# A decoder layer on one core: attention values moved in front of later scores, row sums of two halves grouped, five short reorderings

## Chip, cores and metric

The kernel runs on one core of a Trainium2 chip. The time is the device time of one execution in microseconds (us), lower is better; a comparison is made over the median of several runs of each kernel on the same chip. The core has five engines that run their own queues in order: PE (matmuls; PEld is its weight load), DVE (vector), ACT (scalar), POOL and SP, the last two used mainly to issue transfers. PE writes its results to PSUM, eight banks of 2 KB in each of 128 partitions; DVE and ACT read them there.

## What is computed

One layer of a decoder for 512 tokens of width 1024, batch 1, all in float32. Cut to what matters:

```
mod = silu(c) @ w_ada + b_ada                 # 6 rows of 1024: shift, scale, gate for two halves of the layer
h = rmsnorm(x) * (1 + scale1) + shift1
q, k, v, qd, kd, vd, ga, gd = split(h @ w_in)
out_a = sliding-window attention, 8 heads in blocks of 128, sink term in the softmax, ALiBi
out_d = differential attention, 4 heads, two softmax maps each, per-head rmsnorm
merged = sigmoid(ga) * (out_a @ w_branch_swa) + sigmoid(gd) * (out_d @ w_branch_diff)
x = x + gate1 * (merged @ w_out)
h2 = rmsnorm(x) * (1 + scale2) + shift2
a, g = split(h2 @ w_up);  a = causal depthwise conv of width 3 of a
x = x + gate2 * ((gelu(a) * g) @ w_down)
return rmsnorm(x) * final_g
```

## The kernel before

**Precision.** Most products are made from a high part and a low part of each operand (three matmuls in place of one). The high part is a cast on ACT, the low part a subtraction on DVE (`split`, `cast_w` and `low_w`). So each weight block costs one DMA, one ACT and one DVE instruction before PE can use it. `raw`, `whi` and `wlo` tiles have a few buffers each and are given back when their readers are done.

**Who orders what.** A planner orders the instructions of each engine from the program's order, priorities and estimated durations, and picks the buffer of each tile. Inside `manual_schedule` the named engines keep the program's order. PE is held so through the whole of attention, while DVE and ACT are not; from the end of the output projection (L1283) to L1480 all four of PE, DVE, ACT and POOL are held, and again in `last_rows` at the very end.

**Attention.** PE's program is a line of projection steps (`fill(n)` runs n steps; a step is three matmuls of 512 columns) with the pieces of attention set in between at fixed places. Sliding heads are worked two at a time, as pairs 0 to 3, by the loop at L843: scores of the next pair (`swa_scores`), transpositions of this pair's probabilities in two halves (`swa_transpose`, one for each head of the pair, each in two tiles), softmax of the next pair on DVE and ACT (`swa_softmax`), then the values of this pair (`swa_values`). The values are sixteen matmuls `oa` (L606); ACT (L428) and DVE (L429) take the result out of PSUM into `outa`. Scores end in DVE's reduction (L561), softmax in DVE's scaling of the probabilities by the inverse sums (L584), which the transpositions read (L595).

**PSUM banks.** Four tags: `f` (2 banks, projections), `s` (3, scores), `t` (2, transpositions, row sums and small things), `v` (1, values, and the second scores of the second half in a pair). A tile waits until the former user of its bank has been read.

**Modulation rows.** `ada_rows` makes four of the six rows of `mod` beside attention, with one 512 KB load each eighth fill step: DVE multiplies weight rows by silu(c) and adds them up in an accumulator `arow` (L776, L778), one for each half of a row. When a half is complete, `ada_spread` sums it over the partitions by four column groups of matmuls with ones (`pr`, L789), ACT copies the result (`row`, L794) and POOL issues the write to `mod_rows` in memory (L795). Later steps read the rows from there.

**Up projection.** `w_up` is applied in a scheme with seven products in place of eight (names `p1`, `p2`, `p3`, `p4`, `m5`, `m6`, `m7`) for each pair J of column blocks. `mul_slot(J, name)` is a product of 24 matmuls (L1150), `sum_w` makes a sum of weights on DVE in place, `cast_w` and `low_w` make its high and low part, `behind(J, name)` takes a product out of PSUM, and `conv_bias`, `conv_taps` and `conv_gelu` do the convolution: ACT, then two DVE operations, then ACT. For J = 0, 1 and the begin of 2 the order is written out by hand (L1368 to L1479), from J = 2 on a loop runs over the slots. In front of it, `turn2` transposes normalised rows into the two `t` banks, and `mod_one` (ACT) reads them into `b12` and `b22`.

**Down projection and end.** The same scheme in passes over `w_down`, each with six groups of weights and two row blocks u = 0, 1 (`multiply(i, g, u)`, L1759). The pass `m7` and the last pass `p4` add into the same two banks; between the two, DVE reads the banks (L1633). The last three groups of `p4` are in `last_rows`: block 0 completely, block 1 in two halves of columns `c0` and `c1`, and then the final rmsnorm of the two blocks: multiply, add, squares on ACT, inverse root (`rstd_start` on DVE and POOL, `rstd_end` on DVE), scale, store.

Of the kernel before, what the change touches and what calls it, by code (L numbers as in the profile page):

```python
# [14 lines left out]
P = 128  # L15
# [38 lines left out]
def kernel(  # L54
# [47 lines left out]
    def vbank(name):  # L102
        return bank("v", 1, [P, S], name)
# [410 lines left out]
    def after(n, fn):  # L514
        later.append([n, fn])
# [82 lines left out]
        c.pT.append(pt)  # L598

    def swa_values(i):  # L600
        o = vbank(f"oa{i}")
        for kb in (0, 2, 1, 3):
            w = P if kb == 3 else 2 * P
            for j in range(2):
                rows = slice(64 * j, 64 * j + 64)
                nc.tensor.matmul(  # L606
                    o[rows, kb * P : kb * P + w], va[:, kb, rows],
                    pairs[i].pT[j][:, kb * 256 : kb * 256 + w],
                    start=kb == 0, stop=kb == 3, tile_position=(0, 64 * j),
                )  # L610
        with tc.high_priority(offset=HP):
            evac(outa[0][:, i], outa[1][:, i], o)
# [144 lines left out]
    def ada_load(idx, hf, k):  # L757
        c0 = (2 + idx) * D + hf * S
        r = raw_tile([P, 2, S], f"ra{idx}{hf}_{k}")
        nc.sync.dma_start(r, wada[k * P : (k + 2) * P, c0 : c0 + S].rearrange("(a p) n -> p a n", p=P))  # L760
        return r


    def ada_rows():
        todo = [(idx, hf, k) for idx in range(4) for hf in range(2) for k in range(0, KT, 2)]
        r = ada_load(*todo[0])
        yield
        for (idx, hf, k), job in zip(todo, todo[1:] + [None]):
            nxt = ada_load(*job) if job else None
            if k == 0:  # L770
                ac = big.tile([P, S], F32, tag=("sq2", "g2b1")[hf], name=f"arow{idx}{hf}")
            with tc.high_priority(offset=HP // 2) if tick[0] > ADA_EASY else ExitStack():
                for a in range(2):
                    cc = cs[:, k + a : k + a + 1]
                    if k + a == 0:
                        nc.vector.tensor_scalar_mul(ac, r[:, a], cc)  # L776
                    else:
                        nc.vector.scalar_tensor_tensor(ac, r[:, a], cc, ac, ALU.mult, ALU.add)  # L778
            if k == KT - 2:
                after(ADA_LAG, lambda idx=idx, hf=hf, ac=ac: ada_spread(idx, hf, ac))  # L780
            r = nxt
            yield


    def ada_spread(idx, hf, ac):
        pr = tbank(f"pr{idx}{hf}", (P, P))
        for g in range(4):
            gs = slice(32 * g, 32 * g + 32)
            nc.tensor.matmul(  # L789
                pr[gs], ones[:, gs], ac[:, g * P : (g + 1) * P], start=True, stop=True, tile_position=(0, 32 * g)  # L790
            )
        row = big.tile([P, P], F32, tag="g2b0", name=f"row{idx}{hf}")
        with tc.high_priority(offset=HP):
            nc.scalar.copy(row, pr)  # L794
        nc.gpsimd.dma_start(  # L795
            mod_rows[idx, hf * S : (hf + 1) * S].rearrange("(g n) -> g n", g=4), row[0:P:32]
        )


    pair_w = {}  # L800
# [42 lines left out]
    for i in range(SWA_PAIRS):  # L843
        more = i + 1 < SWA_PAIRS
        fill(SWA_FILL[3])
        if more:
            swa_scores(i + 1, range(NT))
        swa_transpose(i, 0)
        fill(SWA_FILL[4])
        swa_transpose(i, 1)  # L850
        fill(SWA_FILL[5])
        if more:
            with tc.issue_after(pairs[i].copied.ins):
                swa_softmax(i + 1)
        fill(SWA_FILL[6])
        swa_values(i)
        fill(SWA_FILL[7])
    while units or loaded or current:
        fill(1)
# [397 lines left out]
    def ks(g):  # L1257
        return slice(2 * (g % 2), 2 * (g % 2) + 2)
# [108 lines left out]
    g22 = pairs2.rearrange("p (b u n) -> p b u n", b=2, u=2)  # L1367
    tps = {g: turn2(2, g) for g in (0, 1)}  # L1368
    mul_slot(0, "p2", (0,))
    cast_w(0, "m5")  # L1370
    for g in (0, 1):
        for kk in range(2):
            mod_one(b12[:, ks(g)], tps[g], g, kk)
    for g in (2, 3):
        tps[g] = turn2(2, g)
    mul_slot(0, "p2", (1,))
    mul_slot(1, "p1", (1,))
    mul_slot(1, "p2")
    bV += [tbank("up6"), tbank("up7")]
    low_w(0, "m5")  # L1380
    for q in (q0, q1):
        V.tensor_sub(t1n[:, q], b11[:, q], b12[:, q])
    sum_w(0, "m6")
    hi_t(0, t1n, q0)
    for kk in range(2):
# [47 lines left out]
    mul_slot(1, "m6")  # L1433
    behind(1, "m5")
    conv_bias(0, 1)
    conv_taps(0, 0)
    sum_w(1, "p3")
    conv_taps(0, 1)
    cast_w(1, "p3")
    conv_gelu(0, 0)  # L1440
    behind(1, "m6")
    cast_w(1, "m7")
    low_w(1, "p3")
    mul_slot(1, "p3")
    conv_gelu(0, 1)
    low_w(1, "m7")
# [2 lines left out]
    cast_w(2, "p1")  # L1449
    behind(0, "c22")  # L1450
    behind(0, "p4")
    behind(1, "p2")
    low_w(2, "p1")
    mul_slot(2, "p1")
    behind(1, "p3")
    cast_w(1, "p4")
# [238 lines left out]
    def last_rows(todo):  # L1695
        man = ExitStack()
        man.enter_context(
            tc.manual_schedule(engines={nc.vector.engine, nc.scalar.engine, nc.tensor.engine, nc.gpsimd.engine})
        )
        c0, c1 = slice(0, H), slice(H, S)  # L1700
        part = [partial(parts[2 + u, 1]) for u in range(2)]
        for g in todo:
            multiply(len(passes) - 1, g, 0)
        for sl in (c0, c1):
            for g in todo:
                multiply(len(passes) - 1, g, 1, sl)
        for u in range(2):
            nc.scalar.activation(x1[:, u], x1[:, u], AF.Copy, scale=stat_end(u))
            nc.sync.dma_start(od[u * P : (u + 1) * P, :], x1[:, u])
        last_mul(0)  # L1710
        s0 = last_add(0)
        last_gain(0)
        last_mul(1, c0)
        r0 = rstd_start(s0, 1, D, bp, plus=part[0])
        s1 = last_add(1, c0)
        last_gain(1, c0)
        rs0 = bp.tile([P, 1], F32, tag="rs2", bufs=4, name="rse0")
        rstd_end(rs0, *r0, 1, bp)
        partial(s1, part[1])
        last_mul(1, c1)  # L1720
        s2 = last_add(1, c1)
        r1 = rstd_start(s2, 1, D, bp, plus=s1)
        last_gain(1, c1)
        last_scale(0, rs0)
        last_scale2(0, rs0, nc.sync)
        rs1 = bp.tile([P, 1], F32, tag="rs2", bufs=4, name="rse1")
        rstd_end(rs1, *r1, 1, bp)
        last_scale(1, rs1)
        last_scale2(1, rs1, nc.scalar)
        man.close()  # L1730
# [37 lines left out]
    for i in range(len(passes)):  # L1768
        for g in range(NG):
            prepare(i, g)  # L1770
            for _ in range(EACH.get(i, (0,) * NG)[g]):
                next(tasks)()
        tail = HOLD if i == len(passes) - 1 else 0
        for g in range(NG - tail):
            for u in range(2):
                multiply(i, g, u)
        if tail:
            last_rows(range(NG - tail, NG))
        else:
            tasks = after_pass(passes[i][0])  # L1780
            if i < 2:
                for _ in tasks:
                    pass
# [27 lines left out]
```

## Time and profile before

| | us |
|---|---|
| median of 3 runs | 704.18 (704.02 to 706.19) |
| profiled execution | 704.88 |
| its span, first to last instruction | 703.0 |
| PE busy | 683.2 (97%) |
| PE's weight loads busy | 595.3 (85%) |
| DVE busy | 571.9 (81%) |
| ACT busy | 375.5 (53%) |
| POOL busy | 82.3 (12%) |

The profile is of one execution. Its rows give the start in us from the begin of the span, the length, the engine, the line of the kernel, the operation, the tile written and the tiles read, the shape and a count of merged instructions; a bracket gives the engine's idle time in front of the row and what ended it. Matmuls overlap, so the length of one is more than its share of PE's time; the distance of starts is what counts. Rough places in time: norm and the sliding heads' projection to 60 us, sliding heads to 119, differential heads, gates and merge to 316, output projection to 362, up projection to 588, down projection to 694, end to 703.

### The profile page before, as it was taken

The page shows a single profiled execution, that of the slowest core. Times are in us where ns is not written, and L with a number is a line of the kernel's source. Part 1 is how long each engine was busy: PE and PEld are TensorE (multiplying, and loading weights), DVE is VectorE, ACT ScalarE, POOL GpSimd, SP SyncE. Part 2 cuts the span into 40 slices and gives each one's busy share as a digit, 9 for nine tenths or more (in the row PEclk, how much of TensorE's full clock was granted, in tenths as well). Part 3 has the DMA queues.
Part 4 walks back from the last instruction along what each step waited for, and adds up shares of the span by engine and source line. Part 5 has one row for each costly group of instructions (what it writes and reads, how often), then busy time and mean ns, then how long its engine had stood idle before and what let it go on. Part 6 is the DMA issues. An engine that isn't in the chain of part 4 may idle for free. (4 is left out here: it accounts for less than half of the span.)

```text
span 703.0 us, 11254 instructions
## 1 busy us (share of the span) xinstructions
PE 683.2 (97%) x4203; PEld 595.3 (85%) x4203; DVE 571.9 (81%) x1098; ACT 375.5 (53%) x668; POOL 82.3 (12%) x100
## 2 busy tenths in 40 slices
PE   6999999999999999999999999999999999999994
PEld 5777776778788888888889999999999999888884
DVE  5899886887885557664589898888888999979996
ACT  3646767455452333331468566655565666656664
POOL 3000000001001000000030111111111102530300
PEclk9999999999999999999999999999999999999998
DMA  9885454354435676229517798786889647996803
GB/s 312 282 260 174 150 151 151 92 170 128 134 108 158 194 225 202 96 106 275 185 44 149 188 212 204 169 206 194 197 213 231 156 148 204 196 198 192 157 1 119
DMA packets 115862, 121.81 MB, mean 173 GB/s; under 512 B 4383, under 2 KB 93280, under 8 KB 115808
## 3 DMA queue, kind: packets, MB, share of 16 engines
q1 hardware_dynamic: 96894, 95.09, 42.5%
q0 software_dynamic: 18720, 25.73, 21.7%
q8 instruction: 33, 0.54, 0.3%
q10 hardware_dynamic: 194, 0.28, 0.1%
q14 instruction: 21, 0.17, 0.1%
HBM read 118.97 MB, written 2.11 MB: 172 GB/s over the span
## 5 line engine op out<-in xcount | busy, mean ns | idle before, releaser
L1150 PE MATMUL up<-t,m_whi 128*128 128x256 f32 x528 | 96.1, 283 | 0.0
L1150 PEld LDWEIGHTS up<-t,m_whi 128*128 128x128 f32 x528 | 82.4, 192 | 0.0
L1150 PE MATMUL up<-t,m_wlo 128*128 128x256 f32 x264 | 74.7, 283 | 0.1
L1150 PE MATMUL up<-bh,p_wlo 128*128 128x256 f32 x232 | 65.7, 284 | 0.6 <-DVE p_wlo L1093 0.6
L1150 PE MATMUL up<-bh,p_whi 128*128 128x256 f32 x232 | 65.6, 283 | 0.0
L1150 PE MATMUL up<-bl,p_whi 128*128 128x256 f32 x232 | 65.6, 283 | 0.0
L778 DVE SCALAR_TENSOR_TENSOR arow<-ra,cs,arow 128x512 f32<-128x512 f32 x56 | 41.9, 748 | 21.7 <-DMA ra<-in_w_ada_dram 21.3
L1150 PEld LDWEIGHTS up<-t,m_wlo 128*128 128x128 f32 x264 | 50.6, 192 | 0.3 <-DVE m_wlo L1093 0.3
L1150 PEld LDWEIGHTS up<-bh,p_wlo 128*128 128x128 f32 x232 | 44.4, 192 | 1.0 <-DVE p_wlo L1093 1.0
L1150 PEld LDWEIGHTS up<-bl,p_whi 128*128 128x128 f32 x232 | 44.5, 192 | 0.0
L1150 PEld LDWEIGHTS up<-bh,p_whi 128*128 128x128 f32 x232 | 44.5, 192 | 0.0
L1061 POOL DMA_DIRECT2D s<-in_w_up_dram x21 | 27.0, 1360 | 143.2 <-DMA s<-in_w_up_dram 80.9
L1093 DVE TENSOR_TENSOR m_wlo<-s,m_whi 128x1024 fp32r<-128x1024 f32 x31 | 37.7, 1218 | 2.0 <-ACT m_whi L1089 2.0
L1089 ACT CAST m_whi<-s 128x1024 fp32r<-128x1024 f32 x31 | 32.4, 1046 | 9.4 <-DVE s L1083 5.9
L1150 PE MATMUL up<-t,p_whi 128*128 128x256 f32 x176 | 32.2, 283 | 0.0
L173 POOL TENSOR_TENSOR r<-ms,mhalf 128x1 f32<-128x1 f32 (+1 forms) x16 | 12.6, 788 | 134.3 <-DVE ms L171 75.7
L795 POOL DMA_DIRECT2D mod_rows<-row x8 | 5.1, 643 | 196.7 <-ACT row L794 196.7
L1150 PEld LDWEIGHTS up<-t,p_whi 128*128 128x128 f32 x176 | 27.4, 192 | 0.2 <-issue 0.2
L698 ACT ACTIVATE sd<-sd,dmx 128x128 f32<-128x128 f32 (+3 forms) x32 | 17.7, 556 | 18.5 <-DVE dmx L690 18.5
L1157 ACT ACTIVATE gT<-a,cv 128x512 f32<-128x512 f32 x22 | 17.7, 813 | 17.7 <-DVE a L1192 17.3
L1089 ACT CAST p_whi<-wa 128x1024 fp32r<-128x1024 f32 x18 | 18.7, 1040 | 12.0 <-PE up L1150 10.8
L1150 PE MATMUL up<-t,p_wlo 128*128 128x256 f32 x88 | 24.9, 283 | 0.0
(473 smaller groups left out, 2054.1 us busy)
## 6 DMA issues: line engine op xcount, KB each, us to landing
ra<-in_w_ada_dram SPq DMA_DIRECT2D x32, 512.0 KB, 3.9
wa<-in_w_up_dram SPq DMA_DIRECT2D x22, 512.0 KB, 4.1
s<-in_w_up_dram SPq DMA_DIRECT2D x21, 512.0 KB, 4.8
s<-in_w_up_dram POOLq DMA_DIRECT2D x21, 512.0 KB, 7.8
adaw<-in_w_ada_dram SPq DMA_DIRECT2D x16, 512.0 KB, 5.3
w<-in_w_in_dram SPq DMA_DIRECT2D x12, 512.0 KB, 4.0
a<-in_w_up_dram SPq DMA_DIRECT2D x11, 512.0 KB, 4.6
b<-in_w_down_dram SPq DMA_DIRECT2D x10, 512.0 KB, 3.5
```

Of the source, the lines that this page charges most:

```text
L173: nc.gpsimd.tensor_tensor(r0, ms, mhalf[:, :n], ALU.pow)
L698: exp = nc.scalar.activation(pm[m], pm[m], AF.Exp, bias=mx[:, m : m + 1], scale=slope, accum_out=lsum[:, m : m + 1])
L778: nc.vector.scalar_tensor_tensor(ac, r[:, a], cc, ac, ALU.mult, ALU.add)
L795: nc.gpsimd.dma_start(mod_rows[idx, hf * S : (hf + 1) * S].rearrange("(g n) -> g n", g=4), row[0:P:32])
L1061: nc.gpsimd.dma_start(dst, upblock(*blk), accum_op=ALU.add)
L1089: nc.scalar.copy(W[J, name][0], R[J, SRC[name]])
L1093: nc.vector.tensor_sub(lo, R[J, SRC[name]], hi.bitcast(F32))
L1150: nc.tensor.matmul(o[u], w[:, k, cu], b[:, k], start=name in ("p1", "m5", "p2") and k == 0 and x == 0, stop=k == 3 and x == 2, skip_group_ ...
L1157: nc.scalar.activation(grow(j), av[J][:, u], AF.Identity, bias=cv[:, 66 + j : 67 + j], scale=cv[:, 44 + j : 45 + j])
```

## The change

Values of pairs 0 and 1 are issued one turn of the loop later, directly in front of the scores of pairs 2 and 3 (two pairs on), and those of pair 2 directly in front of pair 3's. All but the last go to a `t` bank. `ada_spread` waits for both halves of a row and sums them in one group of sixteen matmuls into one bank, with one copy of twice the width and two writes. Five stretches are put in another order: around the first modulations and `cast_w(0, "m5")`; the sum, high and low part of `p3` of J = 1; the low part of `p1` of J = 2; the end's operations; and the last two groups of pass `m7`, which go over u = 0 first and then over u = 1.

```diff
     def swa_values(i):
-        o = vbank(f"oa{i}")
+        o = (vbank if i == SWA_PAIRS - 1 else tbank)(f"oa{i}")
...
         todo = [(idx, hf, k) for idx in range(4) for hf in range(2) for k in range(0, KT, 2)]
+        sums = [None, None]
...
-            if k == KT - 2:
-                after(ADA_LAG, lambda idx=idx, hf=hf, ac=ac: ada_spread(idx, hf, ac))
+            sums[hf] = ac
+            if hf and k == KT - 2:
+                after(ADA_LAG, lambda idx=idx, acs=tuple(sums): ada_spread(idx, acs))
...
-    def ada_spread(idx, hf, ac):
-        pr = tbank(f"pr{idx}{hf}", (P, P))
-        for g in range(4):
-            gs = slice(32 * g, 32 * g + 32)
-            nc.tensor.matmul(
-                pr[gs], ones[:, gs], ac[:, g * P : (g + 1) * P], start=True, stop=True, tile_position=(0, 32 * g)
-            )
-        row = big.tile([P, P], F32, tag="g2b0", name=f"row{idx}{hf}")
+    def ada_spread(idx, acs):
+        pr = tbank(f"pr{idx}", (P, 2, P))
+        for hf, ac in enumerate(acs):
+            for g in range(4):
+                gs = slice(32 * g, 32 * g + 32)
+                nc.tensor.matmul(
+                    pr[gs, hf], ones[:, gs], ac[:, g * P : (g + 1) * P], start=hf == 0, stop=hf == 1,
+                    tile_position=(0, 32 * g), skip_group_check=True,
+                )
+        row = big.tile([P, 2, P], F32, tag="g2b0", name=f"row{idx}")
         with tc.high_priority(offset=HP):
             nc.scalar.copy(row, pr)
-        nc.gpsimd.dma_start(
-            mod_rows[idx, hf * S : (hf + 1) * S].rearrange("(g n) -> g n", g=4), row[0:P:32]
-        )
+        for hf in range(2):
+            nc.gpsimd.dma_start(
+                mod_rows[idx, hf * S : (hf + 1) * S].rearrange("(g n) -> g n", g=4), row[0:P:32, hf]
+            )
...
         if more:
+            if i:
+                swa_values(i - 1)
             swa_scores(i + 1, range(NT))
...
-        swa_values(i)
+        if not more:
+            swa_values(i - 1)
+            swa_values(i)
...
     mul_slot(0, "p2", (0,))
-    cast_w(0, "m5")
     for g in (0, 1):
         for kk in range(2):
             mod_one(b12[:, ks(g)], tps[g], g, kk)
+        if g == 0:
+            cast_w(0, "m5")
...
+    V.tensor_sub(t1n[:, q0], b11[:, q0], b12[:, q0])
     low_w(0, "m5")
-    for q in (q0, q1):
-        V.tensor_sub(t1n[:, q], b11[:, q], b12[:, q])
+    V.tensor_sub(t1n[:, q1], b11[:, q1], b12[:, q1])
...
     conv_bias(0, 1)
+    sum_w(1, "p3")
     conv_taps(0, 0)
-    sum_w(1, "p3")
+    cast_w(1, "p3")
+    low_w(1, "p3")
     conv_taps(0, 1)
-    cast_w(1, "p3")
     conv_gelu(0, 0)
     behind(1, "m6")
     cast_w(1, "m7")
-    low_w(1, "p3")
...
     behind(0, "p4")
+    low_w(2, "p1")
     behind(1, "p2")
-    low_w(2, "p1")
...
         last_gain(0)
-        last_mul(1, c0)
         r0 = rstd_start(s0, 1, D, bp, plus=part[0])
-        s1 = last_add(1, c0)
-        last_gain(1, c0)
         rs0 = bp.tile([P, 1], F32, tag="rs2", bufs=4, name="rse0")
         rstd_end(rs0, *r0, 1, bp)
-        partial(s1, part[1])
+        last_scale2(0, rs0, nc.sync)
+        last_mul(1, c0)
+        s1 = last_add(1, c0)
         last_mul(1, c1)
         s2 = last_add(1, c1)
+        last_scale(0, rs0)
+        partial(s1, part[1])
         r1 = rstd_start(s2, 1, D, bp, plus=s1)
+        last_gain(1, c0)
         last_gain(1, c1)
-        last_scale(0, rs0)
-        last_scale2(0, rs0, nc.sync)
...
         tail = HOLD if i == len(passes) - 1 else 0
-        for g in range(NG - tail):
+        twins = 2 if i == len(passes) - 2 else 0
+        for g in range(NG - tail - twins):
             for u in range(2):
+                multiply(i, g, u)
+        for u in range(2):
+            for g in range(NG - tail - twins, NG - tail):
                 multiply(i, g, u)
```

## The prediction, made before the changed kernel was seen

> **What bounds the kernel now.** I first read the table of stretches (busy time of each engine, with counts), since it says where a gain can still lie.
>
> ```profile
> 60.00:120.00 60.00, 59.15 (x397) 45.53 (x396) 51.12 (x161) 39.25 (x113) 0.77 (x1) 1.00 0.50 153
> 120.00:360.00 240.00, 239.90 (x1202) 193.89 (x1201) 165.67 (x340) 94.68 (x185) 14.58 (x19) 1.00 0.50 155
> 360.00:420.00 60.00, 58.97 (x478) 57.55 (x477) 56.05 (x86) 43.59 (x72) 10.52 (x9) 1.00 0.74 165
> 420.00:660.00 240.00, 240.00 (x1722) 227.60 (x1721) 215.28 (x306) 143.28 (x210) 47.75 (x42) 1.00 0.83 194
> 660.00:703.00 43.00, 33.87 (x163) 28.16 (x161) 35.33 (x64) 23.63 (x40) 2.36 (x4) 0.93 0.23 69
> ```
>
> The columns after the length are PE, PEld, DVE, ACT, POOL, then the granted clock. PE is the bound from 60 us to the end of its work: it is busy 59.15 of 60, 239.90 of 240, 58.97 of 60 and 240.00 of 240 us, at full clock. What can be won before 694 us is therefore PE's small waits (0.85 us in 60-120, 1.03 us in 360-420) and whatever makes PE take longer for the same matrix work. DVE is second, and in 360-420 it is close (56.05 of 60). Behind PE's last matmul lies a chain of other engines up to the end; there the bound is latency. I then read PE's timeline around every place the diff touches, and after it DVE and ACT there.
>
> **Row sums in one group.** One island of eight small matmuls (four column groups, two passes) stands between projection matmuls:
>
> ```profile
> 108.82 0.40 PE L121 MATMUL pw<-hThA,w_l 128*128 128x512 f32 x1
> 109.14 0.43 PE L789 MATMUL pr<-arow,ones 128*32 128x128 f32 x8
> ...
> 109.83 0.39 PE L120 MATMUL pw<-hTlA,w_h 128*128 128x512 f32 x1
> 110.06 0.40 PE L121 MATMUL pw<-hThA,w_l 128*128 128x512 f32 x1
> ```
>
> Projection matmuls start 0.23 us apart (109.83 to 110.06). From 108.82 to 109.83 are two such steps plus the island: 1.01 - 0.46 = 0.55 us, most of which is getting in and out. There are eight islands now (2 halves x 4 rows) and four of double size afterwards. The added eight matmuls cost at least nothing and at most the 0.43 us that eight take from first start to last end; I take the middle, 0.22, because four of the eight overlap in one pass. New: 4 x 0.77 = 3.08 us, old: 8 x 0.55 = 4.40 us. Term **-1.3** (bounds -2.2 and -0.5). The copies fall from eight to four, each wider, on an ACT that has 145 of 240 us free; the eight write-outs stay eight, two at a time on POOL's queue, which is busy 0.77 of 60 us, then 14.58 of 240. Their first reader is the gate row after attention; if that cover went, two queued issues would cost a microsecond there. The first accumulator is now held until the second is full, so the next row's first product on DVE has one ada step of room, not five; at this pace that is eight fill steps, and I count it at nothing.
>
> **Values in front of the scores.** First the price of such a group alone, then joined to scores, then scores alone:
>
> ```profile
> 79.00 0.39 PE L121 MATMUL pw<-hThA,w_l 128*128 128x512 f32 x1
> ...
> 81.31 0.40 PE L120 MATMUL pw<-hTlA,w_h 128*128 128x512 f32 x1
> ...
> 116.77 0.40 PE L121 MATMUL pw<-hThB,w_l 128*128 128x512 f32 x1
> 117.09 1.73 PE L606 MATMUL oa<-pT,va 128*64 128x256 f32 x16
> ...
> 119.98 0.40 PE L120 MATMUL pga<-hTlA,wga_h 128*128 128x512 f32 x1
> ...
> 138.71 0.40 PE L121 MATMUL pA<-outah,wba_l 128*128 128x512 f32 x1
> ...
> 140.26 0.40 PE L120 MATMUL pA<-outal,wba_h 128*128 128x512 f32 x1
> ```
>
> Alone: 81.31 - 79.00 - 0.46 = 1.85 us. Last pair, whose scores follow directly: 119.98 - 116.77 - 0.46 = 2.75, less scores alone 140.26 - 138.71 - 0.46 = 1.09, makes 1.66. Joining is worth 0.19, and three groups get joined (pairs 0 and 1 to scores, pair 2 to pair 3): **-0.57** (bounds 0 and -0.8).
>
> [...]
>
> **The two waits next to it.** The values leave PSUM's single v bank by ACT and then DVE, and the next scores need that bank:
>
> ```profile
> 84.60 1.79 PE L126 MATMUL sw<-ka,qa 64*128 64x128 f32 x24
> 86.33 0.87 PE L595 MATMUL tp<-ident,st 128*128 128x128 f32 x6
> ...
> 97.41 1.07 PE L126 MATMUL sw<-ka,qa 64*128 64x128 f32 x13
> ...
> 99.60 0.98 PE L595 MATMUL tp<-ident,st 128*128 128x128 f32 x7
> ...
> 111.45 0.40 PE L121 MATMUL pw<-hThA,w_l 128*128 128x512 f32 x1
> 112.49 0.65 PE L595 MATMUL tp<-ident,st 128*128 128x128 f32 x4 [0.64 <-ACT row L794]
> ```
>
> The scores at 97.41 take 2.19 us to the next transposition, those at 84.60 took 1.73: 0.46 lost. The transpositions at 112.49 stand 1.04 behind the last matmul, where 0.23 is normal: 0.81 lost, because one of the two t banks still held row sums. Both causes go: **-1.27**. What is late next is the softmax of the last pair:
>
> ```profile
> 108.29 1.07 DVE L584 TENSOR_SCALAR st<-st,lsum 128x128 f32<-128x128 f32 x4
> ...
> 111.67 0.34 DVE L584 TENSOR_SCALAR st<-st,lsum 128x256 f32<-128x256 f32 x1
> ```
>
> Those transpositions were due at 111.68. Ahead of them vanish pair 2's values (1.85), one row-sum island (0.55), 0.38 for two joined groups and the 0.46: due at 108.44, while DVE ends the scaling that they read at 108.29 + 1.07 = 109.36. That gives a new wait of 0.92; the second half ends at 112.01 and may add some 0.4, or, if DVE gets its scores sooner, both shrink to nothing. **+0.9** (bounds 0 and +1.6).
>
> **The new price, a t bank held by values.** Transpositions of the same pair come 1.7 us behind the values now, and their second bank is the one with the values in it:
>
> ```profile
> 83.43 0.49 DVE L776 TENSOR_SCALAR arow<-ra,cs 128x512 f32<-128x512 f32 x1 [1.73 <-DMA ra<-in_w_ada_dram]
> ...
> 84.70 0.66 DVE L429 TENSOR_TENSOR outal<-oa,outah 128x512 fp32r<-128x512 f32 x1
> ```
>
> Before, pair 0's values ended at about 81.0 and DVE released their bank at 84.70 + 0.66 = 85.36, over 4 us later, behind a row product that sat 1.73 us for its DMA. Scores (1.73) and one transposition group (0.44) cover 2.2 us of such a lag, twice (pairs 0 and 1). In the new place ACT is idle and the DVE wait at 83.43 already over, so ACT's copy and DVE's subtraction, some 1.3 us, fit: **0**, with 2 x 2.1 us if the lag stays as it was (a rival below). What queues behind a late subtraction on DVE is the score reduction, which feeds the next softmax.
>
> **Reorderings around the up projection.**
>
> ```profile
> 368.36 1.23 DVE L1093 TENSOR_TENSOR m_wlo<-s_t,m_whi 128x1024 fp32r<-128x1024 f32 x1 [0.76 <-ACT m_whi L1089]
> ...
> 399.54 1.23 DVE L1093 TENSOR_TENSOR m_wlo<-s,m_whi 128x1024 fp32r<-128x1024 f32 x1 [2.01 <-ACT m_whi L1089]
> ```
>
> ```profile
> 395.04 1.05 ACT L1089 CAST p_whi<-s 128x1024 fp32r<-128x1024 f32 x1 [2.71 <-DVE s L1083]
> ...
> 397.93 0.63 ACT L1186 COPY a<-up 128x256 f32<-128x256 f32 x2
> ```
>
> ```profile
> 397.58 0.39 PE L1150 MATMUL up<-bh,p_wlo 128*128 128x256 f32 x1 [0.31 <-DVE p_wlo L1093]
> ```
>
> This PE wait is for the low half of `p3` of pair 1, which the new order makes earlier, as it does that of `p1` of pair 2. Yet DVE is full here, so removing PE waits is worth only the idle time that DVE itself loses, chiefly the 2.01 us before 399.54. With the sum ahead of the first taps (two tap operations, about 1.4 us), the cast at 395.04 and ACT's row behind it move up 1.4; then the copies of 397.93 wait for PE's product, which is there at about 397.1, so they and the cast behind them come some 0.7 sooner. Against that, swapping `cast_w(0, "m5")` behind the first two modulations delays DVE: the first subtraction (0.6) fills part of the 0.76, but the low half then waits for a cast that ends 0.9 later, and the row comes out about 0.2 to 0.3 behind. The second bank of the third and fourth transposition groups frees no sooner, since both modulations and the cast are ahead of it either way. Moving `low_w(2, "p1")` ahead of two adds leaves DVE's total as it is. **-0.4** (bounds +0.3 and -1.5).
>
> **Last two passes and tail.**
>
> ```profile
> 678.05 0.39 PE L1759 MATMUL dc<-m7wh,m7a 128*128 128x512 f32 x1
> 678.63 0.47 PE L1759 MATMUL dc<-p4wh,p4a 128*128 128x512 f32 x1 [0.19 <-DVE chain_outl L1633]
> ```
>
> ```profile
> 692.28 0.61 ACT L1677 ACTIVATE sqe<-x 128x512 f32<-128x512 f32 x1
> ```
>
> ```profile
> 694.10 0.42 DVE L1671 TENSOR_TENSOR pairs<-dc,g2b 128x256 f32<-128x256 f32 x1 [1.45 <-PE dc L1759]
> 694.44 0.15 DVE L171 SCALAR_TENSOR_TENSOR ms<-sse,ssd 128x1 f32<-128x1 f32 x1
> ...
> 695.68 0.16 DVE L183 SCALAR_TENSOR_TENSOR rse<-rt,r 128x1 f32<-128x1 f32 x1
> ...
> 696.33 0.42 DVE L1674 TENSOR_TENSOR x<-x,pairs 128x256 f32<-128x256 f32 x1
> 697.38 0.16 DVE L171 SCALAR_TENSOR_TENSOR ms<-sse,sse 128x1 f32<-128x1 f32 x1 [0.63 <-ACT sqe L1677]
> ```
>
> Twin order in `m7` finishes its first bank 1.4 us sooner, so the 0.58 - 0.23 = 0.35 us between 678.05 and 678.63 go. But the tail then hangs on another chain: the first row block's square ends on ACT at about 693.0, its inverse root takes 694.44 to 695.84 = 1.40 (POOL's power in it), so DVE is free for the last block's first half at about 694.4, not before, whatever PE wins. I count the 0.35 at nothing. From there four operations 0.45 apart (mul, add, mul, add) reach the last add at 695.75, where 696.33 stands now: 0.6 sooner, and with it the last root, scale and stores. Then the stores:
>
> ```profile
> 699.00:700.00 1.00, 0.00 (x0) 0.00 (x0) 0.28 (x1) 0.52 (x1) 0.00 (x0) 0.50 1.04 401
> ```
>
> The DMA engines are full (share 1.04) while four blocks leave together; two of them now leave some 2 us sooner, so the last two have the engines to themselves. I take 0.3 for it. **-0.9** (bounds +0.4, if DVE's rows are pushed back by a later weight cast in the twin pass, and -1.5).
>
> [...]
>
> **Sum.** -1.3 - 0.57 - 1.27 + 0.9 - 0.4 - 0.9 = -3.5 us. The profiled execution took 704.88 us (span 703.0 and 1.9 around it), 0.7 over the median of 704.18. Taken from its own time: 701.3 for a profile like it; from the median: **700.6 us**.
>
> **Rivals.**
> (a) The bank lag stays. If DVE releases the values 4.3 us after PE, as at 85.36, the second transposition group waits 2.1 us in each of two pairs, and the scaling of the last pair comes later by as much as one of these, 2.1 - 0.9 = 1.2 over the wait I count. It decides from a lag of 2.2 us on. For it: DVE waits on ada DMAs throughout this stage and its order is set by a planner. Against: that wait was over when the new place comes. -3.5 + 4.2 + 1.2 = +1.9: **706.1**, slower. Chance 0.1.
> (b) Only gains behind 120 us and in the tail survive, since scores, softmax and transpositions of a pair form one chain through DVE (51.12 of 60 us busy). Then the row sums from 120 us on (seven islands, 3.85, against four, 3.08) give 0.8 and the tail 0.9: **702.5**, same. For it: the 0.92 wait above. Against: DVE still has 9 us free there. Chance 0.15.
> (c) The grouping doesn't do what it says: the second half of the sums waits for the first to leave its column groups, nothing is won, and the joined values cost their seam: -3.5 + 1.3 + 0.57 = -1.6, **702.6**, same. Chance 0.08.
>
> **Chances and range.** My forecast holds with 0.67; its own range is 698.6 to 702.4. With the rivals on the upper side the range is 698.3 to 704.0; (a) lies outside, and a little of (b). About 0.3%, 2.1 us, is what can be told from no change: faster means under 702.1. Faster 0.68 (most of the forecast, a little of b and c), same 0.21, slower 0.11.
>
> **What would show it.** Four groups of sixteen at the row-sum line, each about 0.77 us between projection matmuls; no wait of scores for the values' low half; a PE wait for DVE in front of the last pair's transpositions; DVE's idle time before the second `m7` low half shorter than 2.01; the last add of the tail about 0.6 nearer to PE's end. It is wrong if transpositions wait for the values' release, if PE loses as much in 360-420 as now, or if PE waits at the seam from `m7` to `p4`.

## The result, and the profile after

The changed kernel takes **710.25 us** (median of six runs, 707.98 to 712.95) where the kernel before takes 704.4 beside it: ratio 1.0071, 95% interval 1.0048 to 1.0093. It is slower by 3.4 to 6.6 us, where 3.5 us faster was forecast and the range ended at 704.0. The profiled execution is the fastest of the six, 707.98 us with a span of 706.0; the others had a lower mean granted clock (0.993 down to 0.988; more stretches of half clock like those of the last section, each 1.71 us or 0.0024 of the span short of full clock, would do that, but none of these executions has a profile). So what follows accounts for the 3.1 us between the two profiled executions (704.88 and 707.98); where the rest of the 5.85 us between the medians falls is not shown.

The table of stretches, with the columns of the prediction's first fence:

```profile
60.00:120.00 60.00, 57.25 (x381) 45.17 (x380) 47.26 (x156) 37.67 (x108) 0.00 (x0) 0.97 0.45 136
120.00:360.00 240.00, 235.50 (x1188) 190.95 (x1187) 164.58 (x337) 93.54 (x176) 14.51 (x19) 1.00 0.52 157
360.00:420.00 60.00, 58.37 (x463) 56.42 (x462) 55.72 (x88) 43.37 (x74) 11.46 (x10) 1.00 0.68 154
420.00:660.00 240.00, 240.00 (x1739) 228.35 (x1738) 215.30 (x304) 142.60 (x207) 45.66 (x40) 1.00 0.82 193
660.00:706.00 46.00, 38.00 (x182) 31.86 (x180) 39.05 (x72) 26.53 (x46) 4.70 (x6) 0.95 0.33 84
```

PE was busy 59.15 of the 60 us from 60 to 120 and now 57.25, at a granted clock of 0.97; it was busy 239.90 of 240 from 120 to 360 and now 235.50. PE idles 6.3 us more in these two stretches. The stage from 420 to 660 is unchanged. The view of PE's waits names three of about 2 us that the kernel before does not have (total, times, longest):

```profile
PE tp L595 <- DVE outal L429: 2.2, 1, 2.2
PE sd L126 <- DVE qkv L429: 2.2, 1, 2.2
...
PE td L716 <- DVE dls L701: 1.8, 1, 1.8
```

To set kernels beside each other although their starts differ, I read the start of the first matmul of five tiles on PE's timeline and took the distances (us): sliding scores `sw` to differential scores `sd`, from there to the small transposition `pm` behind attention, to the first `up`, to the first `dc`, to PE's last matmul, to the end of the span.

| profiled execution | sw to sd | sd to pm | pm to up | up to dc | dc to PE's end | tail |
|---|---|---|---|---|---|---|
| before | 55.88 | 198.22 | 45.63 | 225.86 | 105.59 | 8.93 |
| changed | 57.63 | 202.43 | 46.29 | 225.48 | 105.17 | 7.96 |

The loss is +1.75 in the sliding stage and +4.21 in the differential stage; the step from `pm` to `up` loses 0.66, and the last three columns win 0.38, 0.42 and 0.97. (The first scores come at 61.00 after 62.88, in code that the change does not touch.)

**First loss: the bank of the values.** PE's timeline at pair 0:

```profile
80.72 1.73 PE L606 MATMUL oa<-pT,va 128*64 128x256 f32 x16
82.38 1.68 PE L126 MATMUL sw<-ka,qa 64*128 64x128 f32 x24
83.99 0.66 PE L595 MATMUL tp<-ident,st 128*128 128x128 f32 x4
86.86 0.86 PE L595 MATMUL tp<-ident,st 128*128 128x128 f32 x3 [2.22 <-DVE outal L429]
```

and what ACT and DVE did meanwhile:

```profile
82.50 0.59 ACT L428 CAST outah<-oa 128x512 fp32r<-128x512 f32 x1 [1.20 <-PE oa L606]
...
83.34 1.07 DVE L584 TENSOR_SCALAR st<-st,lsum 128x128 f32<-128x128 f32 x4
84.32 0.75 DVE L779 SCALAR_TENSOR_TENSOR arow<-ra,cs,arow 128x512 f32<-128x512 f32 x1
84.98 1.22 DVE L116 TENSOR_TENSOR w_l<-w,w_h 128x1024 fp32r<-128x1024 f32 x1
86.12 0.68 DVE L429 TENSOR_TENSOR outal<-oa,outah 128x512 fp32r<-128x512 f32 x1
```

ACT has its copy at 83.09. DVE could subtract then and does so at 86.12, behind a scaling, a row product and the low half of a weight. The second transposition group needs that bank and stands 2.22 us.

**Second loss: the held accumulators.** DVE's timeline, then PE's:

```profile
104.99 0.74 DVE L779 SCALAR_TENSOR_TENSOR arow<-ra,cs,arow 128x512 f32<-128x512 f32 x1
...
136.38 0.49 DVE L777 TENSOR_SCALAR arow<-ra,cs 128x512 f32<-128x512 f32 x1 [0.74 <-PE pr L792]
...
145.53 0.48 DVE L777 TENSOR_SCALAR arow<-ra,cs 128x512 f32<-128x512 f32 x1
145.92 0.28 DVE L703 TENSOR_SCALAR sd<-sd,dls 128x128 f32<-128x128 f32 x1
146.12 0.75 DVE L779 SCALAR_TENSOR_TENSOR arow<-ra,cs,arow 128x512 f32<-128x512 f32 x1
146.78 0.35 DVE L704 SCALAR_TENSOR_TENSOR sd<-sd,dls,sd 128x128 f32<-128x128 f32 x1
...
164.61 0.75 DVE L779 SCALAR_TENSOR_TENSOR arow<-ra,cs,arow 128x512 f32<-128x512 f32 x1
165.27 0.68 DVE L429 TENSOR_TENSOR qkv<-pk,qkv 128x512 fp32r<-128x512 f32 x1
```

```profile
135.88 0.65 PE L792 MATMUL pr<-arow,ones 128*32 128x128 f32 x16
...
147.27 0.30 PE L716 MATMUL td<-ident,sd 128*128 128x128 f32 x1 [1.80 <-DVE dls L701]
...
166.01 0.85 PE L126 MATMUL sd<-qkv 64*128 64x128 f32 x10 [2.18 <-DVE qkv L429]
```

Between 105.7 and 136.4 there is no row product at all; both accumulators wait for the group at 135.88. Then sixteen follow up to 165.4, among the operations of the differential softmax and in front of the low half of the keys. PE waits 1.80 and 2.18 us for those: 3.98 of the 4.21 us.

### The profile page after: what moved, and what is told of

Same layout as the page of the kernel before. It is cut to its first block, busy times and chain, and to the rows that moved or that the text cites. A ratio compares the mean times of both kernels' runs of the same rounds, so it can differ in the third digit from the quotient of the medians.

```text
span 706.0 us, 11250 instructions
## 1 busy us (share of the span) xinstructions
PE 679.8 (96%) x4203; PEld 593.8 (84%) x4203; DVE 572.2 (81%) x1098; ACT 376.8 (53%) x664; POOL 82.6 (12%) x100
```

## Experiments

All kernels of this section compute the whole layer. Each stands beside the kernel before on the same chip. The m5 swap is the first of the five reorderings, the one around `cast_w(0, "m5")`.

| run | us, median | before beside it | ratio, 95% interval |
|---|---|---|---|
| e1 values alone | 705.48 | 704.3 | 1.0017 (1.0008 to 1.0027) |
| e2 row sums alone | 711.35 | 704.3 | 1.0098 (1.0085 to 1.0111) |
| e3 five reorderings | 702.6 | 704.3 | 0.9982 (0.9968 to 0.9996) |
| e4 row sums, three accumulators | 703.48 | 704.3 | 0.999 (0.9978 to 1.0002) |
| e5 hold without grouping | 710.31 | 704.43 | 1.0081 (1.0066 to 1.0096) |
| e6 values, bank freed by ACT | 704.41 | 704.43 | 1.0 (0.9988 to 1.0012) |
| e7 reorderings without the m5 swap | 702.18 | 704.43 | 0.9971 (0.9961 to 0.9982) |
| e8 all mended | 704.76 | 704.43 | 0.9998 (0.9986 to 1.0011) |
| e9 as e6, pair 2 left in place | 704.2 | 704.28 | 0.9997 (0.9986 to 1.0007) |
| e10 e4 and e7 together | 700.98 | 704.28 | 0.9954 (0.9942 to 0.9967) |
| e11 e10, head values' bank freed by ACT | 701.14 | 704.28 | 0.996 (0.9946 to 0.9974) |
| e12 all mends | 701.17 | 704.28 | 0.9963 (0.995 to 0.9976) |
| e13 the change, three accumulators | 703.57 | 704.72 | 0.999 (0.9978 to 1.0002) |
| e14 the change without the values | 708.57 | 704.72 | 1.0056 (1.0036 to 1.0076) |

### The parts alone: e1, e2, e3

Each takes its own hunks of the diff and nothing else: e1 the bank and the place of `swa_values`, e2 `ada_rows` and `ada_spread`, e3 the rest.

> The values move alone: in front of the scores two pairs on, in a transposition bank; row sums and all five reorderings as before. Main theory (the values' bank is released late by DVE, once, and costs 2.2 us plus a stretch of half clock behind it; a gain of 0.57 for joined groups and 0.46 for the free v bank stands against it): 705.0 to 707.5 us, with a PE wait at the transposition line for DVE outal of about 2 us near 87 us of the span. Rival 1 (the values alone explain the whole loss, as the bank-lag rival of the prediction had it): 709 us or more. Rival 2 (the lag is caused by the row products that the grouping shifted): no such wait, 702 to 704.

> The row sums of both halves in one group alone. Main theory (two accumulators are held until the joint sum, so DVE's row products stand still and then come in runs of sixteen that delay the differential softmax; 4.2 us lost between 120 and 316 us, the 1.3 for the four fewer groups already counted in it): 707.0 to 709.0 us, with no row product on DVE between about 105 and 136 us and PE waits for DVE dls or qkv of about 2 us at two places. Rival 1 (the values' move makes the whole loss): 702.6 to 703.6, the predicted gain of 1.3. Rival 2 (any change of order makes the planner's result worse): 705 to 707, with the waits in other places.

> The five reorderings alone (two passes around the up projection, a low half, the last pass's rows, and the twin order of the last pass but one). Main theory, as predicted: -0.4 in the up projection and -0.9 in the tail, 702.6 to 703.8 us. From the profile after, where the th line waits 0.66 and 0.83 us, the up part may be worth nothing: then 703.3 to 704. Rival (reorderings upset the planner's order and lose what the tail gains): 704.5 or more.

They came at +1.2, +7.05 and -1.7 us by the medians; the sum, +6.5, is the change's +5.85 within its interval. In e1 the second transpositions of pair 0 stand 2.26 us for `outal` although the row sums are as before, so that stall belongs to the values and rival 2 falls:

```profile
88.79 0.55 PE L595 MATMUL tp<-ident,st 128*128 128x128 f32 x3 [2.26 <-DVE outal L429]
```

In e2 the row products stop at 105.1 and start again at 134.94, and the waits for `dls` and `qkv` of 2.0 and 2.2 us are there; it is 2.4 over the 709.0 named, since both are followed by a stretch of half clock (1.71 us short of full clock each, last section). The gain of the reorderings is spread as in the changed kernel: up to dc 225.48, dc to PE's end 105.17, tail 7.95.

### Is it the hold? e4, e5, e13, e14

e4 groups the sums and gives them a third accumulator in turn; the row's copy makes place for it:

```diff
-                ac = big.tile([P, S], F32, tag=("sq2", "g2b1")[hf], name=f"arow{idx}{hf}")
+                ac = big.tile([P, S], F32, tag=("sq2", "g2b1", "g2b0")[(2 * idx + hf) % 3], name=f"arow{idx}{hf}")
...
-        row = big.tile([P, 2, P], F32, tag="g2b0", name=f"row{idx}")
+        row = (big if idx == 3 else ap).tile([P, 2, P], F32, tag="g2b0" if idx == 3 else "rowx", name=f"row{idx}")
```

> The row sums of both halves in one group, with three accumulators in turn instead of two (and the row's copy in another buffer, so that a place comes free), so that the next half can start while two are held. Main theory (the held accumulator is what costs): the joint groups' gain of 1.3 us is left, 702.6 to 703.8 us, with row products on DVE spread again. Rival 1 (the wider copy, or the two write-outs together, cost the time): as with two accumulators, 707 to 709. Rival 2 (the row products come at another point of the softmax whatever the buffers): 704.5 to 707.

e5 does the reverse to the kernel before: eight separate groups, but the first half's waits until the second half is complete.

```diff
+        held = []
...
             if k == KT - 2:
-                after(ADA_LAG, lambda idx=idx, hf=hf, ac=ac: ada_spread(idx, hf, ac))
+                held.append((idx, hf, ac))
+                if hf:
+                    for n, job1 in enumerate(held):
+                        after(ADA_LAG + n, lambda job1=job1: ada_spread(*job1))
+                    held = []
```

> The kernel before with one edit: the sums of a row's first half are issued only when the second half is complete, so the first accumulator is held as long as in the change, but nothing is grouped (eight groups of eight, copies and write-outs as before). Main theory (holding both accumulators is the cost, not the grouping): at least as slow as the grouped sums alone, whose fewer groups still win a little: 711 to 713 us, with no row products on DVE between about 105 and 135 us. Rival (the wide group, its copy or its paired write-outs are the cost): 704 to 706.

DVE's row products in e4:

```profile
104.52 0.74 DVE L779 SCALAR_TENSOR_TENSOR arow<-ra,cs,arow 128x512 f32<-128x512 f32 x1
105.18 0.48 DVE L777 TENSOR_SCALAR arow<-ra,cs 128x512 f32<-128x512 f32 x1
...
121.55 0.75 DVE L779 SCALAR_TENSOR_TENSOR arow<-ra,cs,arow 128x512 f32<-128x512 f32 x1 [1.60 <-DMA ra<-in_w_ada_dram]
...
128.82 0.74 DVE L779 SCALAR_TENSOR_TENSOR arow<-ra,cs,arow 128x512 f32<-128x512 f32 x1
```

and DVE's and PE's in e5:

```profile
134.01 0.49 DVE L777 TENSOR_SCALAR arow<-ra,cs 128x512 f32<-128x512 f32 x1 [0.74 <-PE pr L794]
...
144.95 0.30 PE L716 MATMUL td<-ident,sd 128*128 128x128 f32 x1 [1.53 <-DVE dls L701]
...
163.67 1.44 PE L126 MATMUL sd<-qkv 64*128 64x128 f32 x10 [2.13 <-DVE qkv L429]
```

With a third accumulator the next half starts 0.66 us after the last product of the half before has started, and waits only for its DMAs; 7.9 us of e2 are gone. Holding without any grouping costs nearly all of it: 5.9 us (4.6 to 6.8 by the interval), a little under the 711 to 713 expected. So the hold is the cause; the wide group and its copy are not. (The intervals of e2 and e5 overlap, so the gain that the fewer groups should keep even here is not seen.)

> The whole change with one mend, three accumulators in turn (and the row's copy in another buffer). Main theory (the held accumulator is 7.9 of the loss: 711.35 less 703.48 between the two runs of the sums alone): 710.25 - 7.9 = 702.4, give or take 1.2 us; what is left over the kernel with sums and orders alone (700.98) is the price of the values, 1.2 to 2.5. Rival (in the whole change the values' bank carries a larger part than alone, since both stalls fall on one DVE queue): 704.5 or more.

> The whole change without the move of the values (two accumulators as in the change). Main theory (the held accumulator by itself makes the kernel slower than before; the values add 1.2): 711.35 - 1.7 = 709.0 to 710.2 us. Rival (both parts share one stall, so that taking either away wins the most of the loss): 704 to 707.

In the whole change the third accumulator alone brings 710.25 to 703.57, 6.7 us; taking the values out brings it to 708.57, 1.7 (just under the 709.0 to 710.2 named). Taking one away leaves the price of the other, so the parts do not share one stall. e13 ended 1.2 above the 702.4 named, at the edge of what was allowed. It is 2.6 over e10, which leaves out the values and the m5 swap; some 0.4 of that may be the chip, since the kernel before took 704.72 beside the one and 704.28 beside the other.

### Why the values win nothing: e6, e8, e9, e11, e12

e6 frees the bank by ACT alone and splits from a copy:

```diff
+        oc = ap.tile([P, S], F32, tag="of", bufs=2, name=f"oc{i}")
         with tc.high_priority(offset=HP):
-            evac(outa[0][:, i], outa[1][:, i], o)
+            nc.scalar.copy(oc, o)
+            evac(outa[0][:, i], outa[1][:, i], oc)
```

> The values' move alone as in the run of the values, but ACT copies the bank to SBUF first, and both halves of the split are then made from that copy: the bank is free once ACT is done, wherever DVE stands. Main theory (the transpositions wait for DVE's place in its queue, 2.3 us, and a slow stretch of some 1.3 us follows): no PE wait for outal, full clock near 88 us, 701.5 to 703.5 us, that is the gain for joined groups and the free v bank. Rival (the seam of values, scores and transpositions loses time by itself, or the extra ACT copy delays the softmax): 704 to 706.

The wait for `outal` is gone, and the time is that of the kernel before, 0.9 to 2.9 us over what was expected and inside the rival's range. PE and ACT at the last pair:

```profile
107.72 0.39 PE L121 MATMUL pw<-hThA,w_l 128*128 128x512 f32 x1
109.81 1.19 PE L595 MATMUL tp<-ident,st 128*128 128x128 f32 x7 [1.70 <-DVE lsum L581]
...
109.03 0.56 ACT L428 CAST qkv<-pv 128x512 fp32r<-128x512 f32 x1
109.50 0.26 ACT L796 COPY row<-pr 128x128 f32<-128x128 f32 x1
```

The profile names `lsum`, which no transposition reads. The copy of a row sum ends at 109.76, and the transpositions start at 109.81: again a transposition bank, held by a row sum whose copy stands behind the exponentials on ACT. It is the wait that the kernel before shows as 0.64 at 112.49, now met earlier and longer. The rival's extra copies on ACT are not its cause: ACT stood idle for 3.40 us in front of those exponentials (104.92) and copies no values between them and the row sum. With sums, orders and this mend together (all but the m5 swap) the next holder shows:

> All of the change but the m5 swap, with both mends: three accumulators in turn, and the values' bank freed by ACT's copy. Main theory (parts add up: -0.8 for the sums with three accumulators, -1.5 for the values with their bank free, -2.0 for the orders, as far as these were measured or are expected): 699.5 to 701.5 us, below both kernels and at the prediction. Rival (the mends take each other's place on ACT, or the joined groups bring the last pair's softmax onto PE's path): 702 to 704.

Timeline of e8, PE and DVE:

```profile
111.19 0.55 PE L595 MATMUL tp<-ident,st 128*128 128x128 f32 x3 [3.20 <-DVE qkv L429]
...
108.92 1.54 DVE L781 SCALAR_TENSOR_TENSOR arow<-ra,cs,arow 128x512 f32<-128x512 f32 x2 [1.05 <-DMA ra<-in_w_ada_dram]
...
110.45 0.69 DVE L429 TENSOR_TENSOR qkv<-pv,qkv 128x512 fp32r<-128x512 f32 x1
```

Here the bank holds the transposed values of a differential head, and their low half stands on DVE behind two row products, the first of which waits 1.05 us for its DMA. 704.76 instead of 699.5 to 701.5: a miss too, and over the rival's 702 to 704.

So two more mends: pair 2's values stay between the last pair's softmax and its transpositions (e9, with the v bank for it), and the head values' bank is freed by ACT in the same way (e11 on the kernel without the values' move, e12 with everything).

```diff
-        if not more:
-            swa_values(i - 1)
+        if i >= SWA_PAIRS - 2:
             swa_values(i)
```

```diff
-                evac(t[:, 4], t[:, 5], pv)
+                pc = ap.tile([P, S], F32, tag="of", bufs=2, name=f"pc{h}")
+                with tc.high_priority(offset=HP):
+                    nc.scalar.copy(pc, pv)
+                evac(t[:, 4], t[:, 5], pc)
```

> Values with the bank freed by ACT, but pair 2's values stay where they were, between the last pair's softmax and its transpositions; only those of pairs 0 and 1 move. Main theory (the 1.85 us of values that left this place were the cover of the last pair; without them its transpositions stood 2.09 us at 107.72, until ACT's copy of a row sum freed a transposition bank): that stall falls to about 0.2, with the half clock behind it gone, 702.0 to 703.5 us. Rival (softmax is late by itself and the stall moves on to the second half): 704 to 705.

> As the run before it, and the transposition bank of each differential head's values is freed by ACT alone (a copy to SBUF, split from there), not by DVE's subtraction. Main theory (that subtraction stands behind row products on DVE and holds a transposition bank: 1.10 us lost at 110.31 in the run with three accumulators): that wait goes, 0.7 to 1.1 us faster than without. Rival (the wait passes to the softmax's scaling on DVE, 0.9 later in the prediction): no faster.

> All parts but the m5 swap, with all mends: three accumulators, the values' and the head values' banks freed by ACT, pair 2's values left as cover of the last pair. Main theory (with no transposition bank waiting for DVE, joining is worth the 0.38 and the free v bank the 0.46 of the prediction): 0.5 to 0.9 faster than without the values' move, 699.5 to 701.2 us. Rival (the stage follows the softmax chain on DVE and ACT, and the move of the values is worth nothing even so): equal to the run without it or slower.

e9 stays at the kernel before, e11 and e12 at e10: the times are those of the rivals (e12's 701.17 is just inside the theory's range too, but no faster than e10). The first row is the last pair's transposition in e11, the two below are e12's values of pair 2 and the same transposition:

```profile
110.70 1.14 PE L595 MATMUL tp<-ident,st 128*128 128x128 f32 x7 [0.98 <-DVE st L584]
```

```profile
104.19 1.73 PE L606 MATMUL oa<-pT,va 128*64 128x256 f32 x16 [0.69 <-DVE mx L561]
...
110.25 1.13 PE L595 MATMUL tp<-ident,st 128*128 128x128 f32 x7 [0.70 <-DVE st L584]
```

With every bank free PE waits for the scaling `st` itself, the last step of the softmax on DVE. The sliding stage, sw to sd, takes 55.88 us before, 55.63 in e10, 56.11 in e11, 55.82 in e9 and 55.84 in e12: whatever PE wins there it waits out again. No run made the softmax itself faster, so that it sets the pace of this stage is read from these waits and not shown by an experiment. (Behind it, sd to pm takes 199.20 in e9 where the kernel before takes 198.22; why was not tried.)

### What is left to win: e7, e10

e7 is e3 without the m5 swap (`cast_w(0, "m5")` and `low_w(0, "m5")` back in front); e10 joins it with e4.

> The reorderings without the one of the cast of m5 (which goes back in front of the first two modulations). By the prediction's term (+0.2 to +0.3 for this swap; 0.42 by the wait at the th line in the run of the reorderings) it is faster than the five together by 0.2 to 0.5: 702.1 to 702.5 us at a median of 702.6 for the five, DVE's idle before the m5 low half back at about 0.8 us, the th wait back at 0.42. Rival (the swap makes room that the later passes use): 0.3 slower than the five.

> No move of the values: three accumulators with the joint row sums, and four of the five reorderings (without the m5 swap). Main theory (parts add up: -0.8 and -2.2): 700.8 to 702.0 us. Rival (the gain of the sums with three accumulators, whose interval holds zero, is none): 702.0 to 702.8.

DVE in front of the low half of m5, in e3 and then in e7:

```profile
367.69 0.69 DVE L1381 TENSOR_TENSOR s_t<-braw,braw 128x512 f32<-128x512 f32 x1 [1.11 <-ACT braw L1255]
368.63 1.23 DVE L1093 TENSOR_TENSOR m_wlo<-s_t,m_whi 128x1024 fp32r<-128x1024 f32 x1 [0.24 <-ACT m_whi L1089]
```

```profile
367.64 1.23 DVE L1093 TENSOR_TENSOR m_wlo<-s_t,m_whi 128x1024 fp32r<-128x1024 f32 x1 [0.76 <-ACT m_whi L1089]
```

The swap turns 0.76 us of idle into 1.35. Without it, up to dc takes 224.96 instead of 225.48 (225.86 before). The medians of e3 and e7 differ by 0.42 in the same direction; their intervals overlap, so it is the stage that carries this. **e10 has the lowest median of all**: 700.98 us, 0.9954 of before (0.9942 to 0.9967), 9.3 us under the change. e7 alone is clear of the kernel before as well, and the two intervals overlap, so that the joint sums add anything to the reorderings is not shown.

## Why the prediction was wrong, point by point

| part | forecast | measured, by medians |
|---|---|---|
| row sums | -1.3 | +7.05 (e2); -0.8 with three accumulators (e4, interval holds zero) |
| values, with their waits, the softmax and the bank | -0.94 | +1.2 (e1); 0 with the bank free (e6, e9) |
| orders, up projection and tail | -1.3 | -1.7 (e3); -2.25 without the m5 swap (e7) |
| sum | -3.5 | +5.85 |

**Row sums: the step that failed** is the sentence "the next row's first product on DVE has one ada step of room, not five; at this pace that is eight fill steps, and I count it at nothing". It counted room in the order in which the program issues its steps. DVE runs far ahead of that order, since its products wait for DMAs (before, 21.3 of the 21.7 us of idle time in front of those of L778 end with one). In the kernel before, the last product of the first half is

```profile
79.56 0.75 DVE L778 SCALAR_TENSOR_TENSOR arow<-ra,cs,arow 128x512 f32<-128x512 f32 x1
```

and its sum stands on PE at 109.14, in the prediction's own first fence on the row sums: an accumulator is held 28.8 us after it is full. With one accumulator held so, DVE fills the other; with two it has nothing to fill for 31 us. Both rows were there to be read. The rest of the term was right: the group of sixteen costs 0.77 us as worked out. But even with room, sd to pm falls from 198.22 to 197.96 only (the islands behind 120 us should give about 0.8): in front of 222.10 PE loses 0.51, of which it stands 0.35 for ACT's `ta`. And the sliding stage of e4 is 0.29 longer, with 0.93 lost at 111.52 for the bank of the head values where 0.64 was lost for a row sum. From sw to pm e4 takes 254.13 where the kernel before takes 254.10, so the gain of the grouping itself is not shown.

**The t bank: the second step that failed** is "ACT is idle and the DVE wait at 83.43 already over, so ACT's copy and DVE's subtraction, some 1.3 us, fit: 0". ACT was idle, as said. DVE's wait was over too, but a scaling, a row product and a weight's low half stood in its queue, and the subtraction came 3.0 us behind the copy. Rival (a) had this mechanism and its size (2.1, measured 2.22) with a chance of 0.1; in the changed kernel it came in one of two pairs, in e13 in both (2.39 and 1.14).

**Joined groups and removed waits** (-0.57 and -1.27) did come in the changed kernel: its sliding stage is 1.75 longer although it holds a stall of 2.22 and 1.7 of slow clock behind it, so about 2.2 us were won beside them. Joining is worth more than counted: from the last projection matmul to the transposition, pair 1's joined group takes 3.59 us (96.91 to 100.50), scores alone 2.05 (84.28 to 86.33 before) and values alone 1.85 more, so 0.31 is won where 0.19 was taken. **The softmax of the last pair** (+0.9) did not come there: the scaling ends at 108.73, and the transpositions follow at 110.30 without a wait for it; only 0.53 is lost, for the bank of the head values. PE was late by its stall. But the gains do not last. Without the stall PE comes to the next softmax that much sooner, and waits there: in e9, where no values' bank is in the way, 0.40 us at 99.82 for `st`, 0.69 at 104.87 for `mx` and 0.53 at 111.37 for the head values, and the stage is 55.82 against 55.88. The waits for `st` are the prediction's +0.9, in other places. Rival (b), that scores, softmax and transpositions of a pair form one chain through DVE, fits this stage; it had a chance of 0.15. Rival (c), in which the joint of values and scores is the seam, falls: the group of sixteen took the 0.77 us worked out, and that joint came 0.31 cheaper than the two apart.

**Up projection**: forecast -0.4, with +0.2 to +0.3 from the swap; measured -0.38 in up to dc, with +0.52 from the swap. That the total fits is luck in part: without the swap 0.90 is won (e7), and the swap costs twice what was counted. The waits for the low halves of p3 and p1 are gone, and DVE's idle before the second m7 low half went from 2.01 to 0.93. The stage before it, pm to up, is 0.66 longer in the changed kernel, 0.24 in e3 and 0.05 in e13, which have the same edits there. In the changed kernel 0.50 of it is a wait of the transpositions `th` for DVE's `xn` at 362.28; why that varies was not tried. **Tail**: forecast -0.9, measured -0.97. Its rows on DVE:

```profile
696.92 0.16 DVE L171 SCALAR_TENSOR_TENSOR ms<-sse,ssd 128x1 f32<-128x1 f32 x1 [0.33 <-ACT sqe L1687]
...
698.14 0.42 DVE L1681 TENSOR_TENSOR pairs<-dc,g2b 128x256 f32<-128x256 f32 x1
...
699.38 0.42 DVE L1684 TENSOR_TENSOR x<-x,pairs 128x256 f32<-128x256 f32 x1
```

The last add ends 1.80 us behind PE's end (698.00), where it was 2.69. So 0.89 comes from the rows on DVE, for which 0.6 was counted, and 0.08 from what follows, where 0.3 was counted for stores that no longer share the DMA engines (share 1.04, 1.01 and 0.50 in the stretches of 1 us from 699 to 702 before, 0.84 and 0.52 from 703 to 705 now): the two errors cancel, which is luck. The twins, counted at nothing, gave 0.42 on top: the root of the first block now starts 1.08 ahead of PE's end, so an earlier PE is not held up by it.

## What to carry to other kernels

How long a buffer is held is read from the trace, from its last write to the read that frees it, not from the order in which the program issues steps: here DVE, whose row products waited for DMAs, filled an accumulator 28.8 us before PE's sum freed it. An operand kept for a later joint step needs one buffer more, or the producer stops and then comes in a burst where the queue is needed (here 31 us without a row product, then sixteen of them; a third accumulator brought 7.9 us back). And a PSUM bank that is freed by an operation in a busy in-order queue is free when that queue gets there (here 3.0 us behind ACT's copy); before work is moved into a shared bank, list every holder, for each that is mended uncovers the next, and ask whether the chain behind them sets the pace anyway.

## What the runs showed of the hardware

Some PE stalls cost more than their own length here: a stretch of half clock followed them. Stretches of 1 us behind the 2.22 us stall of the changed kernel (the last three columns are the granted clock, the DMA share and GB/s):

```profile
86.00:87.00 1.00, 0.14 (x1) 0.14 (x2) 1.00 (x5) 0.00 (x0) 0.00 (x0) 0.97 0.04 10
87.00:88.00 1.00, 1.00 (x5) 0.90 (x5) 1.00 (x9) 0.24 (x1) 0.00 (x0) 0.50 0.13 17
88.00:89.00 1.00, 1.00 (x4) 0.80 (x3) 1.00 (x7) 0.24 (x1) 0.00 (x0) 0.50 0.85 278
89.00:90.00 1.00, 1.00 (x3) 0.68 (x3) 1.00 (x5) 0.07 (x1) 0.00 (x0) 0.50 0.95 223
90.00:91.00 1.00, 1.00 (x9) 0.92 (x8) 0.22 (x1) 1.00 (x2) 0.00 (x0) 0.82 0.04 6
```

What is missing to full clock adds up to 0.03 + 3 x 0.50 + 0.18 = 1.71 us, that is 3.42 us at half. In that stretch projection matmuls start 0.43 us apart (87.94 to 88.37), at full clock 0.23 (91.45 to 91.68). The same 1.7 follows the 2.26 us stall of e1, both stalls of e2 (2.0 and 2.2), the 2.13 of e5, the 1.70 at 109.81 in e6 and the 3.20 of e8. It follows the 2.2 of e14 as well. It does not follow the 1.80 and 2.18 of this same execution, the 1.53 of e5, the 2.4 of e13 or the 2.0 of e14. Of thirteen stalls of 1.5 us and more behind 60 us, eight were followed by it; the 2.22 us of the changed kernel then cost 3.93. Windows of 60 to 240 us between 60 and 660 us that hold no such stretch have a granted clock of 1.00; of e14 only 138 to 172 us are known.

Why some stalls are followed by the slow clock and others are not stays open.
